# Projections out by one level of Strassen's algorithm, with their weight sums made by accumulating transfers

## The chip, the core and the metric

The kernel runs as one program on one core of a Trainium2 chip. The metric is the device time of one execution in microseconds. Five engines work side by side, each through its own list of instructions in order: TensorE (PE, with weight loads shown as PEld), VectorE (DVE), ScalarE (ACT), GpSimd (POOL) and SyncE (SP). They wait for each other by semaphores. In the kernel before, all transfers between HBM and the on-chip memory are issued by SP; a transfer that has to wait for a semaphore holds up all that SP issues behind it.

## The reference

Two layers over a sequence of 1024 tokens with 1024 features, all in float32:

```
layer 0 (mLSTM):      proj = x @ w_in  ->  xm, o_pre, z, gates        # inner width E = 2048, 4 heads
                      xc = silu(causal conv of xm); q, k from xc, v from xm; h = mLSTM cell
                      y = (sigmoid(o_pre) * norm(h) * gn_w + skip * xc) * silu(z)
                      branch = y @ w_out                               # 1024x2048 @ 2048x1024
layer 1 (short conv): bg, cg, hx, z = split(x @ w_in);  y = silu(z) * bg * conv(cg * hx)
                      branch = y @ w_out
both layers:          x = LayerNorm(ALPHA * x + branch) * g + b        # ALPHA = 4 ** 0.25
                      x = x + sigmoid(x @ W_g) * (p @ W_p)
```

The change is about the two products `y @ w_out`, one per layer, and about what stands on both sides of them.

## The kernel before

Features lie on the 128 partitions, tokens on the free axis in two halves of 512. A tile is 128x512 float32 (256 KB), and comes from one pool of slots whose names begin with the stage's name: `xm`, `oz` and `at` (layer 0: values and convolution, gates o and z, cell), `outa` (projection out), `ga` (embedding gate), then `b`, `outb`, `gb` for layer 1. A name with P in front is a bank of PSUM.

Every float32 operand is split into two fp32r parts: ACT rounds it (L67, "CAST"), DVE subtracts the rounded part (L70, "TENSOR_TENSOR"). A product is three matmuls (`three`, L80, L81, L82).

The order of the work is written out by hand, as one Python program over generators that are stepped at fixed places. Weights of all stages stand in one `stream`; `take` gives the next one and runs ahead with loads and splits by as many as `ahead` says. Heads 0 to 3 follow each other: value projection and convolution (L346, L365, L367), products O and Z of the gates (L549 to L553), the cell in chunks (L450 loads a row of maxima, L458 and L463 decays, L478 to L485), the norm of the cell. `apply_gates` (L560 to L565) loads `xc` back from HBM (`xcdram`), applies skip and gates, and stores `y` to `ydram`; it runs for `held` items when a head's norm has been drained.

`project` (outa, outb) takes a half of the tokens, then each column half: 16 k-tiles of y and of the weight, four banks, 4 x 16 x 3 matmuls, and adds ALPHA times the residual on eviction (L683). `layer_norm` sums over features by POOL additions (L659, L661) and by matmuls with a matrix of ones (L693); it is stepped inside the next half's projection. `gated` computes per tile of 128 features the gate (8 k-tiles), then the embedding product (2 k-tiles), then sigmoid (L784), product and sum (L785, L786). In `ga` each result goes to `keep`, which stores it and makes the operands of stage b.

Stage b, the input projection of layer 1, is already done by Strassen's algorithm in Winograd's form: seven products instead of eight for a 2x2 block product. Its 32 groups of weight rows each have seven products of 4 tiles x 3 matmuls; the weights' sums are made by DVE (L866), the moving operands' sums by `keep` (L819). Products are `a11`, `a12`, `s2`, `s1`, `s3`, `s4`, `a22`; their moving operands are called `n11`, `b21`, `t2`, `t1`, `n3`, `n22`, `n4`. `prepare_products` loads and splits three products ahead (`LEAD`), and starts when stage b starts. `outb` starts its loads when b is over (`fence`: they read what b stores).

Of the kernel before, what the change touches and what calls it, by code (L numbers as in the profile page):

```python
# [13 lines left out]
P = 128  # L14
# [16 lines left out]
AHEAD = {"load": 4, "split": 2}  # L31
LATE = {"load": 4, "split": 2}
# [4 lines left out]
def trunk(ctx: ExitStack, tc: tile.TileContext, I, out: bass.AP):  # L37
# [47 lines left out]
    ydram = dr.tile([16, 2, P, HALF], F32, name="ydram")  # L85
    ybdram = dr.tile([16, 2, P, HALF], F32, name="ybdram")
    mdram = dr.tile([32, P], F32, name="mdram")
    x2dram = dr.tile([8, 2, P, HALF], F32, name="x2dram")

# [13 lines left out]
    for h in range(2):  # L103
        for c in range(2):
            for k in range(16):
                if c == 0:
                    stream.append(("ya", ydram[k, h]))
                stream.append(("woa", I["woa"][cols(k), cols(c, HALF)]))
    for h in range(2):
        for c in (range(8) if h == 0 else ORDER):  # L110
            stream += [("wga", I["wga"][c, j]) for j in range(2)]
    for h in range(2):
        for c in range(2):
            for k in range(16):
                if c == 0:
                    stream.append(("yb", ybdram[k, h]))
                stream.append(("wob", I["wob"][cols(k), cols(c, HALF)]))
# [5 lines left out]
    fence = [[what for what, _ in stream].index("yb")]  # L123
# [228 lines left out]

    for hd in range(HEADS):
# [188 lines left out]
        def project_gates(c, mid):  # L542
# [3 lines left out]
            for h in range(2):  # L546
# [3 lines left out]
                mid()  # L550
                acc = in_group(wz, xsplit, h, mid)
# [3 lines left out]
                mid()  # L555

        def apply_gates(c, h, so, sz):
# [7 lines left out]
            nc.sync.dma_start(ydram[ct, h], sz)  # L565

        held = []

# [71 lines left out]
        if hd == HEADS - 1:  # L640
            ahead.update(load=16, split=3)

        def settle():
            if not step(side) and held:
                apply_gates(*held.pop(0))
# [4 lines left out]
        for item in held:  # L650
            apply_gates(*item)
# [11 lines left out]
    def project(h, ysp, wkind, residual, r, total):  # L663
        ysplit = [None] * 16
        for c in range(2):
            res = []
            acc = [bank() for _ in range(4)]
            for k in range(16):
                if c == 0:
                    ysplit[k] = ysp(k)  # L670
                wh, wl = take(wkind)
                if k == 8:
                    for t in range(4):
                        x = slot()
                        nc.sync.dma_start(x, residual(4 * c + t, h))
                        res.append(x)
                for t in range(4):
                    three(acc[t], (wh[:, cols(t)], wl[:, cols(t)]), ysplit[k], k == 0, k == 15)
                if c == 1:
                    ysplit[k] = None  # L680
                yield
            for t in range(4):
                nc.vector.scalar_tensor_tensor(out=res[t], in0=res[t], scalar=ALPHA, in1=acc[t],  # L683
                                               op0=ALU.mult, op1=ALU.add)
                r.append(res[t])
                summed(total, res[t])

    def summed_rows(stationary, x):
        parts = split(x, "act", "dve")
        yield  # L690
        acc = bank()
        for n in range(2):
            mm(acc, stationary, parts[n], start=(n == 0), stop=(n == 1))  # L693
        return acc

    def layer_norm(layer, h, r, total, x, xs):
        mu = yield from summed_rows(mean, total[1])
# [8 lines left out]
        for _ in range(3):  # L706
            yield
        var = bank()
        for j in range(4):
            mm(var[:, cols(j, 4)], squares[1][:, cols(j)], ones[:, :4], start=True, stop=True)  # L710
        rt = small([P, 4], "rt")
        nc.vector.tensor_scalar(out=rt, in0=var[:, :16].rearrange("p (j c) -> p j c", c=4)[:, :, 0],
                                scalar1=1.0 / DM, scalar2=LN_EPS, op0=ALU.mult, op1=ALU.add)
        nc.gpsimd.tensor_tensor(out=rt, in0=rt, in1=mhalf, op=ALU.pow)
        diag = slot()
# [3 lines left out]
        for _ in range(2):  # L719
            yield  # L720
        rs = yield from summed_rows(onesr, diag)
        yield
# [30 lines left out]
    def both_halves(layer, ysp, wkind, residual, late, early):  # L753
        x, xs = grid(8, 2), grid(8, 2)
        rs, totals = [[], []], [[], []]
        for n, _ in enumerate(project(0, ysp(0), wkind, residual, rs[0], totals[0])):
            if n == 29:
                early()
        side = layer_norm(layer, 0, rs[0], totals[0], x, xs)
        for n, _ in enumerate(project(1, ysp(1), wkind, residual, rs[1], totals[1])):  # L760
            if n % 2:
                step(side)
            if n >= 20:
                step(late)
        drain(side)
        drain(late)
        return x, xs, layer_norm(layer, 1, rs[1], totals[1], x, xs)

    def gated(layer, wkind, x, xs, pw, pt, side, emit):

        more = second_pt(layer, pt)
        for h in range(2):
            for c in (range(8) if h == 0 else ORDER):
                w = take2(wkind)
                acc = in_group(w, xs, h, lambda: step(side))
                step(side)
# [21 lines left out]
    part[0] = "ga"  # L798

# [284 lines left out]
```

## Time and profile before

| what | value |
|---|---|
| median of 3 runs | 2012.98 us (2012.39 to 2015.74) |
| the profiled execution | 2014.51 us, span 2012.7 us, mean granted clock 0.992 |
| PE busy | 1979.2 us, 98%, 8924 matmuls |
| DVE, ACT, POOL busy | 68%, 39%, 10% |
| layer 0 up to its projection out | 0 to 801.5 us |
| outa | 801.5 to 979.8 us |
| ga | 979.8 to 1099.8 us |
| b | 1099.8 to 1717.1 us |
| outb | 1717.1 to 1896.5 us |
| gb | 1896.5 to 2012.7 us |

The stages overlap on the other engines; the borders are those of PE's first matmul of each. A row of a group gives busy time and mean duration of one instruction, then the idle time before it and what ended it. A row of waits reads "engine, line, what it waited for: us in total, times, longest". A row of a window reads "from:to, length, then busy time and count of PE, PEld, DVE, ACT and POOL, PE's granted clock, busy share of the DMA engines, GB/s". A row of the timeline reads "start, duration, engine, line, operation, output<-input, shapes, count [idle before, and what ended it]". A row of DMA issues gives the median time from issue to landing.

### The profile page before, as it was taken

Reading aid. Unit: us, or ns where it says so; the run is one execution under the profiler, and the core shown is the slowest. Engines: PE = TensorE matmul, PEld = TensorE weight load, DVE = VectorE, ACT = ScalarE, POOL = GpSimd, SP = SyncE. Lnnn points to the kernel's source line nnn. Section 1 sums busy time; section 2 is a strip of 40 time slices with the busy share of each in tenths; the row PEclk is TensorE's granted clock in tenths of the full one; section 3 lists DMA queues with packets and bytes.
Section 4 is the critical chain, followed back from the end, with each engine's and each line's share of the span. In section 5 each row is a group of like instructions: output and inputs, shape, how many; then the busy total and the mean of one; then the engine's idle time right before and its main releaser. Section 6 shows DMA issues by size and latency. Waiting matters only on the chain.

```text
span 2012.7 us, 24481 instructions
## 1 busy us (share of the span) xinstructions
PE 1979.2 (98%) x8924; PEld 1631.9 (81%) x8924; DVE 1376.3 (68%) x2310; ACT 778.5 (39%) x1433; POOL 194.8 (10%) x154
## 2 busy tenths in 40 slices
PE   9999999999999999999998999999999999899998
PEld 6788878878887888887886888888888888787887
DVE  7974897589659965636777676676676676537663
ACT  5453235333433443514454333333333323514451
POOL 0210012001201120012300000000000000013200
PEclk9999999999999999999999999999999999999999
DMA  4111311232122123845023212211221220944222
GB/s 155 59 32 64 115 53 32 81 101 64 30 93 101 42 69 133 306 144 165 32 94 126 71 55 66 87 58 58 85 67 53 89 69 16 355 152 143 69 82 84
DMA packets 106058, 188.70 MB, mean 94 GB/s; under 512 B 11441, under 2 KB 15697, under 8 KB 105937
## 3 DMA queue, kind: packets, MB, share of 16 engines
q1 hardware_dynamic: 105936, 187.14, 28.1%
q8 instruction: 70, 1.15, 0.2%
q14 instruction: 52, 0.42, 0.1%
HBM read 153.52 MB, written 33.57 MB: 93 GB/s over the span
## 4 chain that ended last, share of the span: by engine, by line
PE 94%; DVE 4%; DMA 1%; issue 1%; ACT 0%; SPq 0%; DVEq 0%; ACTq 0%
PE Pb L80 10%; PE Pb L81 10%; PE Pb L82 10%; PE Poz L82 5%; PE Poz L80 5%; PE Poz L81 5%; PE Pat L80 3%; PE Pat L82 3%; PE Pat L81 3%; PE Poutb L80 3%; PE Poutb L82 3%; PE Pouta L82 3%; PE Poutb L81 3%; PE Pouta L80 3%; PE Pouta L81 3%; PE Pxm L80 3%
## 5 line engine op out<-in xcount | busy, mean ns | idle before, releaser
L80 PE MATMUL Pb<-ga,b 128*128 128x512 f32 x896 | 349.8, 390 | 6.8 <-ACT b L67 6.8
L81 PE MATMUL Pb<-ga,b 128*128 128x512 f32 x896 | 349.6, 390 | 0.0
L82 PE MATMUL Pb<-ga,b 128*128 128x512 f32 x896 | 347.1, 390 | 0.0
L80 PEld LDWEIGHTS Pb<-ga,b 128*128 128x128 f32 x896 | 168.7, 188 | 41.9 <-ACT b L67 7.2
L82 PEld LDWEIGHTS Pb<-ga,b 128*128 128x128 f32 x896 | 168.6, 188 | 35.2 <-DVE b L70 0.4
L81 PEld LDWEIGHTS Pb<-ga,b 128*128 128x128 f32 x896 | 168.6, 188 | 34.9
L70 DVE TENSOR_TENSOR b<-b,b 128x512 fp32r<-128x512 f32 x224 | 148.6, 687 | 60.5 <-ACT b L67 59.3
L67 ACT CAST b<-b 128x512 fp32r<-128x512 f32 x224 | 130.3, 616 | 113.9 <-DVE b L866 112.7
L911 ACT ACTIVATE b<-Pb 128x512 f32<-128x512 f32 x96 | 57.4, 598 | 203.3 <-PE Pb L82 203.3
L82 PE MATMUL Poz<-start,oz 128*128 128x512 f32 x288 | 115.8, 402 | 6.1 <-DVE oz L70 6.0
L80 PE MATMUL Poz<-start,oz 128*128 128x512 f32 x288 | 116.5, 404 | 0.0
L81 PE MATMUL Poz<-start,oz 128*128 128x512 f32 x288 | 115.2, 400 | 0.0
L80 PE MATMUL Poutb<-outb,outb 128*128 128x512 f32 x256 | 100.8, 394 | 6.3 <-ACT outb L67 6.3
L67 ACT CAST outb<-outb 128x512 fp32r<-128x512 f32 x116 | 67.2, 618 | 88.0 <-POOL outb L661 38.7
L82 PE MATMUL Poutb<-outb,outb 128*128 128x512 f32 x256 | 100.5, 393 | 0.7 <-DVE outb L70 0.7
L81 PE MATMUL Poutb<-outb,outb 128*128 128x512 f32 x256 | 100.4, 392 | 0.0
L82 PE MATMUL Pouta<-outa,outa 128*128 128x512 f32 x240 | 93.9, 391 | 0.8 <-DVE outa L70 0.8
L80 PE MATMUL Pouta<-outa,outa 128*128 128x512 f32 x240 | 93.7, 390 | 0.0
L81 PE MATMUL Pouta<-outa,outa 128*128 128x512 f32 x240 | 93.5, 390 | 0.0
L70 DVE TENSOR_TENSOR outb<-outb,outb 128x512 fp32r<-128x512 f32 x116 | 83.0, 763 | 13.3 <-ACT outb L67 13.0
L964 DVE TENSOR_TENSOR b<-Pb,b 128x512 f32<-128x512 f32 x32 | 22.1, 691 | 101.3 <-PE Pb L82 101.3
L67 ACT CAST outa<-outa 128x512 fp32r<-128x512 f32 x100 | 57.0, 618 | 81.9 <-POOL outa L661 38.7
(356 smaller groups left out, 4462.2 us busy)
## 6 DMA issues: line engine op xcount, KB each, us to landing
b<-wb SPq DMA_DIRECT2D x128, 256.0 KB, 2.9
outb<-wob SPq DMA_DIRECT2D x64, 256.0 KB, 5.3
outa<-woa SPq DMA_DIRECT2D x56, 256.0 KB, 3.8
oz<-wa SPq DMA_DIRECT2D x48, 256.0 KB, 3.6
xm<-wa SPq DMA_DIRECT2D x32, 256.0 KB, 3.0
oz<-xcdram SPq DMA_DIRECT2D x32, 256.0 KB, 3.0
ydram<-oz SPq DMA_DIRECT2D x32, 256.0 KB, 2.0
ybdram<-b SPq DMA_DIRECT2D x32, 256.0 KB, 2.1
```

The lines of the kernel that those rows point to most:

```text
L67: nc.scalar.copy(hi, src)
L70: (nc.vector if lo_on == "dve" else nc.gpsimd).tensor_tensor(out=lo, in0=src, in1=hi.bitcast(F32), op=ALU.subtract)
L80: mm(acc, lh, rh, start=first, stop=False, skip_group_check=onto)
L81: mm(acc, lh, rl, start=False, stop=False, skip_group_check=onto)
L82: mm(acc, ll, rh, start=False, stop=last, skip_group_check=onto)
L911: nc.scalar.activation(t, src, AF.Copy, scale=scale)
L964: nc.vector.tensor_tensor(out=s.c22, in0=acc, in1=s.m5, op=ALU.add)
```

## The change

It does eight things.

1. Both projections out become one Strassen step over 2x2 blocks: token halves, column halves of the weight, and even and odd k-tiles. Class `Out` runs 7 x 8 units of 4 tiles x 3 matmuls (56 units instead of 64), loading four units ahead and splitting two ahead.
2. Their weight sums s1 to s4 are made ahead by `weight_sums`: SP loads one term into a slot, GpSimd adds the other by an accumulating transfer (`add_on`), SP stores the sum to `wsdram`, and `Out` loads it from there. For layer 0 this runs during the O and Z products of heads 1 and 2 (two steps after each half), for layer 1 one step per group of stage b.
3. The moving operands' sums are made by DVE where y is made (`store_moving`), and all seven are stored.
4. The products are added up partly by DVE from PSUM into the residual (`onto`), partly by accumulating transfers between slots. The factor ALPHA moves into 1/ALPHA on the product and into the norm's epsilon.
5. `keep` makes t1 and n4 by accumulating transfers. In all 96 transfers accumulate (two times 32 for weight sums, two times 12 in the projections, 8 in `keep`).
6. The norm's waits are set by a table (`NORM_WAITS`); the embedding products of a half are computed in one block ahead of its gates and evicted by ACT, instead of after each gate.
7. Stage b begins with the first two products of four groups instead of two; its first products, and the first units of both projections, are loaded and split during the stage before.
8. A head's held gates are applied as soon as their part of the norm is there (`apply_ready`).

With it PE's list has 8650 rows instead of 8842, DVE's 2392 instead of 2304, ACT's 1477 instead of 1379, POOL's 255 instead of 159, SP's 925 instead of 717.

The first place is SP's list in head 1, between the last products O and Z before the cell and the cell itself. Before:

```order
L388 DMA xcdram<-xm_2582 128x512
L388 DMA xcdram<-oz_2656 128x512
L450 DMA oz_2814<-mdram 128x4x128
L450 DMA oz_2825<-mdram 128x4x128
L130 DMA at_3258<-wa 128x512
```

And now (L147 loads a term of a sum, L139 stores a sum, L516 is the store to `xcdram`, L578 the load of the maxima):

```order
L516 DMA xcdram<-oz_2693 128x512
L147 DMA oz_2748<-woa 128x512
L147 DMA oz_2749<-woa 128x512
L147 DMA oz_2750<-woa 128x512
L139 DMA wsdram<-oz_2747 128x512
L139 DMA wsdram<-oz_2749 128x512
L139 DMA wsdram<-oz_2748 128x512
L578 DMA oz_2862<-mdram 128x4x128
L578 DMA oz_2873<-mdram 128x4x128
L139 DMA wsdram<-oz_2750 128x512
L256 DMA at_3311<-wa 128x512
```

Three loads and three stores of the sums stand ahead of the cell's first load; the third store is that of s2, which has s1 added to it.

The second place is DVE's list at the boundary of heads 1 and 2. Before (L562 and L564 apply skip and gate, L346 is the next head's convolution):

```order
L553 TENSOR_TENSOR oz_3664<-Poz_3703,oz_3664 128x512
L70 TENSOR_TENSOR xm_3743<-oz_3576,xm_3742 128x512
L70 TENSOR_TENSOR xm_3749<-oz_3582,xm_3748 128x512
L562 SCALAR_TENSOR_TENSOR oz_3663<-oz_3736,cpack,oz_3663 128x512
L564 TENSOR_TENSOR oz_3664<-oz_3664,oz_3663 128x512
L346 SCALAR_TENSOR_TENSOR xm_3781<-xm_3779,cpack,xm_3781 128x511
```

And now (L696 and L698 are the skip and the gate, L94 the sums of `store_moving`, L72 splits, L472 the convolution):

```order
L696 SCALAR_TENSOR_TENSOR oz_3769<-oz_3824,cpack,oz_3769 128x512
L698 TENSOR_TENSOR oz_3770<-oz_3770,oz_3769 128x512
L94 TENSOR_TENSOR oz_3829<-oz_3557,oz_3770 128x512
L94 TENSOR_TENSOR oz_3831<-oz_3557,oz_3452 128x512
L94 TENSOR_TENSOR oz_3833<-oz_3452,oz_3829 128x512
L94 TENSOR_TENSOR oz_3835<-oz_3699,oz_3833 128x512
L72 TENSOR_TENSOR xm_3850<-oz_3690,xm_3849 128x512
L72 TENSOR_TENSOR xm_3856<-oz_3696,xm_3855 128x512
L472 SCALAR_TENSOR_TENSOR xm_3888<-xm_3886,cpack,xm_3888 128x511
```

The four sums now stand between the last gate of a head and the splits and convolution of the next. What L696 reads (`oz_3824`) is a load from `xcdram` that stands in SP's list behind the stores of s1, s3 and s2 of the fourth set.

The third place is ACT's list at the entry into stage b. Before, the first weights' casts (`b_`) stand behind the last gate's work (L784 the sigmoid, L812 a negated operand):

```order
L784 ACTIVATE ga_9707<-Pga_9675 128x512
L67 CAST ga_9716<-ga_9714 128x512
L67 CAST ga_9722<-ga_9712 128x512
L67 CAST ga_9726<-ga_9720 128x512
L812 ACTIVATE ga_9730<-ga_9707 128x512
L67 CAST b_9750<-b_9734 128x512
L67 CAST b_9754<-b_9736 128x512
```

And now (L977 the sigmoid; the first row is the cast of the first weight of stage b, among the last three gates):

```order
L69 CAST ga_9883<-ga_9867 128x512
L69 CAST ga_9887<-ga_9824 128x512
L69 CAST ga_9893<-ga_9830 128x512
L977 ACTIVATE ga_9922<-Pga_9897 128x512
L69 CAST ga_9932<-ga_9929 128x512
```

The cast of the first weight now stands ahead of the sigmoid of the third gate from the end, not behind the last gate's work. The diff, cut to what it is about:

```diff
+INV = 1.0 / ALPHA
+EARLY_GROUPS = 4
...
-    ydram = dr.tile([16, 2, P, HALF], F32, name="ydram")
-    ybdram = dr.tile([16, 2, P, HALF], F32, name="ybdram")
+    ydram = dr.tile([2, 7, 8, P, HALF], F32, name="ydram")
+    wsdram = dr.tile([2, 4, 8, P, HALF], F32, name="wsdram")
...
+    def add_on(dst, src):
+        nc.gpsimd.dma_start(dst, src, accum_op=ALU.add)
...
+    FRESH = ("a11", "a12", "s1")
+    def store_moving(layer, kk, y11, y12, y21, y22):
+        n3 = combined(y12, y22, ALU.subtract)
+        t1 = combined(y12, y11, ALU.subtract)
+        t2 = combined(y11, n3, ALU.subtract)
+        n4 = combined(y21, t2, ALU.subtract)
+        for n, y in enumerate((y11, y21, t2, t1, n3, y22, n4)):
+            nc.sync.dma_start(ydram[layer, n, kk], y)
...
+    def weight_sums(layer, weights):
+        rows = lambda k, i: weights[cols(k), cols(i, HALF)]
+        store = lambda n, kk, t: nc.sync.dma_start(wsdram[layer, n, kk], t)
+        s4 = None
+        for kk in range(8):
+            if s4 is not None:
+                store(3, kk - 1, s4)
+            s1, s2, s3, s4 = (slot() for _ in range(4))
+            for t, src in ((s1, rows(2 * kk, 1)), (s2, rows(2 * kk, 0)), (s3, rows(2 * kk, 0)),
+                           (s4, rows(2 * kk + 1, 0))):
+                nc.sync.dma_start(t, src)
+            yield
+            add_on(s1, rows(2 * kk + 1, 1))
+            add_on(s3, rows(2 * kk, 1))
+            yield
+            add_on(s2, s1)
+            store(0, kk, s1)
+            store(2, kk, s3)
+            s1 = s3 = None
+            yield
+            add_on(s4, s2)
+            store(1, kk, s2)
+            s2 = None
+            yield
+        store(3, 7, s4)
...
+        UNITS = ([("a11", kk) for kk in range(6)] + [("a12", kk) for kk in range(6)]
+                 + [("a11", 6), ("a11", 7), ("a12", 6), ("a12", 7)]
+                 + [(what, kk) for what in ("s2", "s3", "a22", "s1", "s4") for kk in range(8)])
+        LOADS, LEAD = 4, 2
...
+        def load(self, n):
+            while self.loaded < min(n, len(self.UNITS)):
+                for dst, key, src in self.loads[self.loaded]:
+                    dst[key] = slot()
+                    nc.sync.dma_start(dst[key], src)
+                self.loaded += 1
...
+                what, kk = self.UNITS[self.prepared]
+                left = split(self.w.pop((what, kk)), "act", "dve")
+                m = MOVING[what]
+                y = self.y.pop((m, kk))
+                self.ready[what, kk] = left, split_negative(y) if m in NEGATIVE else split(y, "act", "dve")
...
+            for u, (what, kk) in enumerate(self.UNITS):
+                if kk == 7:
+                    continue
+                before(u)
+                self.load(u + 1 + (kk == 6) + self.LOADS)
+                self.prepare(u + 1 + (kk == 6) + self.LEAD)
+                acc = banks(what, kk == 0)
+                for t in range(4):
+                    one(what, kk, t)
+                    if kk == 6:
+                        one(what, 7, t)
+                        after(what, t)
+                        tick()
+                    elif t % 2:
+                        tick()
+                for n in (6, 7) if kk == 6 else (kk,):
+                    del self.ready[what, n]
...
+                if (hd, c, h) == (HEADS - 1, CTH - 1, 1):
+                    outa.prepare(3)
...
+                if hd in (1, 2):
+                    step(sums, 2)
+                if hd == HEADS - 1 and c >= CTH - 2:
+                    outa.load((2, 3, 5, 5)[2 * (c - CTH + 2) + h])
...
-            nc.sync.dma_start(ydram[ct, h], sz)
+            paired[c, h] = sz
+            pair = [(k, l) for k in (c - c % 2, c - c % 2 + 1) for l in range(2)]
+            if all(key in paired for key in pair):
+                store_moving(0, ct // 2, *(paired.pop(key) for key in pair))
...
+        def apply_ready():
+            for n, (c, h, _, _) in enumerate(held):
+                if hnt[h][c] is not None:
+                    apply_gates(*held.pop(n))
+                    return
...
-            if not step(side) and held:
-                apply_gates(*held.pop(0))
+            step(side)
+            apply_ready()
...
+    NORM_WAITS = ((1, 3, 8, 2, 3), (1, 2, 2, 1, 1))
...
+        def onto(r, acc, scale):
+            nc.vector.scalar_tensor_tensor(out=r, in0=acc, scalar=scale, in1=r, op0=ALU.mult, op1=ALU.add)
...
+        def after(what, t):
+            if what == "a11":
+                kept[t] = evacuated(b["b1"][t], -INV)
+            elif what == "a12":
+                r = out_.x[t, 0]
+                onto(r, b["b3"][t], INV)
+                add_on(r, kept.pop(t))
+                b["b3"][t] = None
+            elif what == "s2":
+                result(t, 0)
+                add_on(out_.x[t, 1], evacuated(b["b1"][t], -INV))
+            elif what == "s3":
+                add_on(out_.x[t + 4, 1], evacuated(b["b1"][t], INV))
+            elif what == "a22":
+                add_bank(t + 4, 0, b["b1"][t], INV)
+                b["b1"][t] = None
+            elif what == "s1":
+                add_bank(t + 4, 1, b["b2"][t], INV)
+            else:
+                add_bank(t, 1, b["b2"][t], -INV)
+                b["b2"][t] = None
+        def tick():
+            place[0] += 1
+            if side:
+                step(side[0])
+            elif place[0] >= 2 * 24 and place[0] % 2:
                 step(late)
-        drain(side)
+        out_.run(banks, before, tick, after)
         drain(late)
-        return x, xs, layer_norm(layer, 1, rs[1], totals[1], x, xs)
-
-    def gated(layer, wkind, x, xs, pw, pt, side, emit):
+        return x, xs, side
...
+            embedding = []
+            for c in range(8):
                 pp = bank()
                 for k in range(2):
                     wh, wl = pw[2 * k + c // 4]
                     three(pp, (wh[:, cols(c % 4)], wl[:, cols(c % 4)]), pt[h][k], k == 0, k == 1)
-                step(side)
+                embedding.append(evacuated(pp))
+                del pp
+                if h == 0 and c % 2 == 0:
+                    (fetch if c == 0 else prepare)((4, 2, 3, 4)[c // 2])
+                step(norms[h])
+                if h == 0 and c % 2:
+                    step(norms[1])
+            pt[h].clear()
+            drain(norms[h])
+            if h:
+                pw.clear()
+            for n, c in enumerate(range(8) if h == 0 else ORDER):
...
+            negative[c] = slot()
+            nc.scalar.activation(negative[c], x2, AF.Copy, scale=-1.0)
         elif c < 4:
-            t1 = difference(x2, raw2[k][0])
-            ops["t1"][k] = split(t1, "act", "dve")
+            add_on(negative[k], x2)
+            finish_operands()
...
+            add_on(negative[k + 4], t2)
             ops["t2"][k] = split(t2, "act", "dve")
-            n4 = difference(raw2[k + 4][0], t2)
+            ops["t1"][k] = split(negative.pop(k), "act", "dve")
...
+            def last():
+                ops["n4"][k] = split_negative(negative.pop(k + 4))
+            late.append(last)
...
+        made[c, h] = y
+        if c % 2 and h == 0:
+            store_moving(1, c // 2, *(made.pop((k, h)) for k in (c - 1, c) for h in range(2)))
...
+    def hook(n):
+        if n >= 5:
+            prepare_products(n - 4)
+    gated(0, "wga", x1, x1s, pw, pt, side, keep, hook)
+    part[0] = "b"
+    outb = Out(1, I["wob"], lambda k, h: x2dram[k, h])
+    sums = weight_sums(1, I["wob"])
...
+        if g == len(groups) - 1:
+            outb.load(1 + n)
+            outb.prepare(max(0, n - 3))
         product(g, n)
+        if n == 3 and 0 < g:
+            step(sums)
+    drain(sums)
```

More of the change, by code (lines that the diff above doesn't have):

```diff
@@ L661, in summed, with over_rows @@
             nc.gpsimd.tensor_tensor(out=total[1], in0=total[1], in1=x, op=ALU.add)
[L663 to L690, printed above, removed]
+    def over_rows(stationary, parts):
         acc = bank()
@@ L694, in summed_rows, with waits @@
         return acc
+    NORM_WAITS = ((1, 3, 8, 2, 3), (1, 2, 2, 1, 1))
     def layer_norm(layer, h, r, total, x, xs):
-        mu = yield from summed_rows(mean, total[1])
+        def waits(n):
+            return range(NORM_WAITS[h][n])
+        for _ in waits(0):
+            yield
+        parts = split(total[1], "act", "dve")
+        total.clear()
+        for _ in waits(1):
+            yield
+        mu = over_rows(mean, parts)
+        del parts
         squares = []
@@ L705, in layer_norm @@
                 yield
-        for _ in range(3):
+        del mu
+        for _ in waits(2):
             yield
@@ L718, in layer_norm @@
                                 in1=rt.unsqueeze(2).to_broadcast([P, 4, P]), op=ALU.mult)
[L719 removed]
+        parts = split(diag, "act", "dve")
+        del diag
+        for _ in waits(4):
             yield
[L721 to L722 removed]
+        rs = over_rows(onesr, parts)
+        del parts
         for k in range(8):
@@ L751, in grid, with back, banks, result @@
         return [[None] * m for _ in range(n)]
-    def both_halves(layer, ysp, wkind, residual, late, early):
+    def back(layer, out_, before, late):
         x, xs = grid(8, 2), grid(8, 2)
[L755 to L761, printed above, removed]
-                step(side)
-            if n >= 20:
+        rs, totals, side = [{}, {}], [[], []], []
+        b, kept, place = {}, {}, [0]
+        BANK = {"a12": "b3", "s1": "b2", "s4": "b2"}
+        def banks(what, first):
+            name = BANK.get(what, "b1")
+            if first and what in FRESH:
+                b[name] = [bank() for _ in range(4)]
+            return b[name]
+        def onto(r, acc, scale):
+            nc.vector.scalar_tensor_tensor(out=r, in0=acc, scalar=scale, in1=r, op0=ALU.mult, op1=ALU.add)
+        def result(c, h):
+            r = rs[h][c] = out_.x.pop((c, h))
+            summed(totals[h], r)
+            if len(rs[h]) == 8:
+                side.append(layer_norm(layer, h, rs[h], totals[h], x, xs))
+        def add_bank(c, h, acc, scale):
+            onto(out_.x[c, h], acc, scale)
+            result(c, h)
+        def after(what, t):
[16 more added lines that the diff above has]
+                add_bank(t + 4, 1, b["b2"][t], INV)
+            else:
+                add_bank(t, 1, b["b2"][t], -INV)
[5 more added lines that the diff above has]
+            elif place[0] >= 2 * 24 and place[0] % 2:
@@ L994, in trunk @@
     fence[0] = len(stream)
-    ahead.update(load=16, split=4)
     pw, pt = [], ([], [])
-    x3, x3s, side = both_halves(1, lambda h: lambda k: take("yb"), "wob", lambda k, h: x2dram[k, h],
-                                ple_operands(1, pw, pt, 0), lambda: None)
+    x3, x3s, side = back(1, outb, lambda u: None, ple_operands(1, pw, pt, 0))
     ahead.update(load=4, split=2)
```

141 lines of the change are left out of this document (84 added, 57 removed).

## The prediction

> **What bounds the kernel now.** I read the page first, then the rows of each stretch, the list of PE's waits, the chain around the longest of them, and the DMA issues.
>
> ```profile
> PE 1979.2 (98%) x8924; PEld 1631.9 (81%) x8924; DVE 1376.3 (68%) x2310; ACT 778.5 (39%) x1433; POOL 194.8 (10%) x154
> PE 94%; DVE 4%; DMA 1%; issue 1%; ACT 0%; SPq 0%; DVEq 0%; ACTq 0%
> 1138.90:1700.10 561.20, 561.20 (x2477) 465.05 (x2477) 390.74 (x653) 182.59 (x324) 0.00 (x0) 1.00 0.21 68
> ```
>
> PE is busy 98% of the span and holds 94% of the chain that ended last. The third row is the undisturbed part of stage b: 561.20 us for 2477 matmuls, so a 128x512 matmul advances the end by 561.20/2477 = 0.2266 us. The 390 ns that the groups give as a mean overlap, and are no cost. The kernel therefore takes its matmuls times 0.2266 us plus the places where PE stands still. Those are few:
>
> ```profile
> PE Pb L80 <- ACT b L67: 6.8, 1, 6.8
> PE Poutb L80 <- ACT outb L67: 6.3, 1, 6.3
> PE Poz L82 <- DVE oz L70: 6.0, 3, 2.0
> PE Pouta L82 <- DVE outa L70: 1.0, 3, 0.4
> PE Poutb L82 <- DVE outb L70: 0.7, 2, 0.4
> ```
>
> The columns are total us, times, longest. The first two are the entries into b and outb, the third the three boundaries between heads. All other stages, both projections out included, run at PE's pace.
>
> **Fewer matmuls.** A projection out is now 2 halves x 2 column halves x 16 k x 4 tiles x 3 = 768 matmuls of 128x512. With seven products it is 7 x 8 x 4 x 3 = 672. Two layers: 192 fewer, 192 x 0.2266 = **-43.5 us**. The gates keep their 192 matmuls per half and the embedding its 48; those only stand in another order. Nothing hides this term as long as PE stays the bound there.
>
> **The two entries.** The chain of waits there:
>
> ```profile
> 1092.86 0.24 PE Pga L82
> ...
> 1099.28 0.52 ACT b L67
> ...
> 1099.84 0.80 PE Pb L80
> 1100.63 0.43 PE Pb L81
> ...
> 1712.53 3.86 DMA outb<-wob
> ...
> 1717.09 0.80 PE Poutb L80
> 1717.88 0.43 PE Poutb L81
> ```
>
> Into b, the last gate's result goes through DVE and ACT, and only behind that does ACT cast the first weights. PE stands 6.8 us, and its next five matmuls take 0.43 instead of 0.23 us, 1.6 us with the first one's 0.80. Into outb a weight load is issued only when everything before it is over; 6.3 us, and 1.9 us behind it in the same way. After the change three units of weights are loaded and split ahead at both places, 3 x 12 x 0.2266 = 8.2 us of matmuls that wait for nothing new, and b's first eight products (four groups, a11 and a12: 8 x 12 x 0.2266 = 21.8 us) need only n11 and b21, which the gates of the first half make. I take both as gone: 6.8 + 1.6 + 6.3 + 1.9 = **-16.6 us**. If the cover were short, at most these 16.6 come back.
>
> **The norm.** The mean's sums wait twice in each layer (last two rows, 0.4 at the longest). Placed later by the new pacing they go: 1.0 + 0.7 and their slower restart, **-2 us**. Norm 0 now lies inside the 16 units of s1 and s4, 43.5 us. Per 96 matmuls (21.8 us) the densest part of the new order gives DVE 29 operations of 128x512.
>
> ```profile
> 801.54:979.81 178.27, 177.27 (x781) 145.64 (x780) 101.60 (x152) 73.40 (x130) 27.31 (x19) 1.00 0.55 182
> L70 DVE TENSOR_TENSOR outa<-outa,outa 128x512 fp32r<-128x512 f32 x100 | 70.8, 777 | 7.4 <-ACT outa L67 7.4
> ```
>
> The first row is outa (DVE 101.6 of 178.3 us), the second its splits, 777 ns each. 29 x 0.777 = 22.5 us against 21.8: 0.7 us too much, with a lead of two units (5.4 us) that absorbs it once but not where waits for POOL's sums fall into it. Bounds: 0 with all absorbed, 4 us a layer if the windows beside it (26 operations, 20.2 us) lose two waits of 0.7 each as well. I take 1.5 a layer, **+3 us**.
>
> **The tail.** The embedding's six matmuls (1.4 us) stood behind the last gate and covered its sigmoid. Now the sigmoid stands bare ahead of
>
> ```profile
> 2007.80 0.70 DVE gb L785
> 2008.52 0.69 DVE gb L786
> ```
>
> ACT's 0.6 us and the hand-overs: **+0.8 us**.
>
> **The weight sums.** This is the part whose price the trace does not have. No row of the kernel before is an accumulating transfer, and no transfer starts on GpSimd. Let A be the time from the start of one such 256 KB transfer to its landing. The nearest rows:
>
> ```profile
> b<-wb SPq DMA_DIRECT2D x128, 256.0 KB, 2.9
> outb<-wob SPq DMA_DIRECT2D x64, 256.0 KB, 5.3
> oz<-xcdram SPq DMA_DIRECT2D x32, 256.0 KB, 3.0
> ydram<-oz SPq DMA_DIRECT2D x32, 256.0 KB, 2.0
> outa<-woa SPq DMA_DIRECT2D x56, 256.0 KB, 3.8
> oz<-mdram SPq DMA_DIRECT2D x8, 256.0 KB, 4.2
> ```
>
> From below 2.9, a load in a quiet stage. From above 5.3 + 2.0 = 7.3, a load in the busiest stage and then a store, since what is added to is read and written again. I take the 5.3 between.
>
> The Trainium skill ("DMA: Bandwidth & Descriptors", section "Anatomy of one DMA — SWDGE (gpsimd) path") gives 2.0 us plus bytes over 436 GB/s for a transfer that GpSimd issues, so an estimate of 2.6 us for this size. No run here shows it; with it the two terms below would be zero.
>
> In b a step of the sums comes once in a group (38 us), and a store never waits for an add of its own step: no cost. In heads 1 and 2 two steps come together, so SP issues a store that waits for an add just begun, and everything behind it in SP's order waits too.
>
> Place one is the entry into the cells of heads 1 and 2:
>
> ```profile
> 301.13 0.33 SPq L388 DMA_DIRECT2D xcdram<-oz  x1
> 304.28 1.24 SPq L450 DMA_DIRECT2D oz<-mdram  x2
> ...
> 315.50 0.62 ACT L480 CAST at<-at 128x512 fp32r<-128x512 f32 x1 [0.76 <-DVE at L478]
> ...
> 317.96 0.44 PE L80 MATMUL Pat<-oz,at 128*128 128x512 f32 x1
> ```
>
> Behind the xcdram store at 301.13 SP now issues the loads of s2, s3, s4 (0.4 each), which land 3.8 later, 305.7; GpSimd then adds s1 onto s2, and its store (306 + A) stands before the mdram loads, which land 4.2 and some issue later, 311 + A. ACT began on them at 313.55, and its product has 317.96 - 316.12 = 1.8 us to spare. Stall: 311 + A - 313.5 - 1.8, about A - 4; 1.3 us a head at 5.3.
>
> Place two is the boundary behind heads 1 and 2:
>
> ```profile
> 419.18 2.32 DVE L346 SCALAR_TENSOR_TENSOR xm<-xm,cpack,xm 128x511 f32<-128x511 f32 x3 [2.83 <-ACT xm L376]
> ...
> 440.42 0.69 DVE L387 TENSOR_TENSOR xm<-xm,xm 128x512 f32<-128x512 f32 x1 [0.76 <-ACT xm L381]
> ...
> 452.94 0.50 PE L82 MATMUL Poz<-start,oz 128*128 128x512 f32 x1 [2.01 <-DVE oz L70]
> ```
>
> From the next head's first convolution (419.18) DVE runs with 0.76 us idle until a split for which PE already waits 2.01 us (452.94). So whatever delays that convolution by more than 0.76 goes into the span. In the new order the third set's loads are issued 186 matmuls ahead of that point, at 419.18 - 42.2 = 377.0, and land at 380.8; three adds, each waiting for the one before (380.8 + 3A); the fourth set's first load (1.7 for issue, 3.8 to land), two more adds (386.3 + 5A); two issues and the xcdram load behind them (0.8 + 3.0), then on DVE two operations of the gate, four of store_moving and two splits (5.5) before the convolution: 395.6 + 5A against 419.94. At 5.3: 2.2 us a head; nothing below 4.9. Together 2 x (1.3 + 2.2) = 7 us, and the matmuls behind a stop of 2 us cost another 1.4 each time as at the entries: **+10 us**.
>
> The other side of the two bounds is 0 at A = 2.9 and 2 x (3.3 + 12.1) + 3 = 34 us at 7.3.
>
> Another rule of the Trainium skill speaks against this change ("SBUF — State Buffer", section "Who interferes with whom"): operations of DVE in a two-port mode, tensor_scalar among them, lock GpSimd out while it writes its descriptors. The page reports a transfer of 620 ns that took 3100. No run here shows it; by it A would be longest exactly at place two, where such operations stand in rows.
>
> **The sum.** The profiled execution has a span of 2012.7 us (2014.51 around it; the median of the runs is 2012.98). 2012.7 - 43.5 - 16.6 - 2 + 3 + 0.8 + 10 = 1964.4, so a median of about **1965 us**.
>
> **Rivals.** (1) *The sums are hidden.* A below 4.9 and DVE never late: 1964.4 - 10 - 3 = **1951**. For it speak the 2.9 and 3.0 of the loads in quiet stages; against it, that the sums read two sources and that DVE's part of place two (5.5 us) is longer than the 2.83 idle there. (2) *Slow sums.* A from 6.5 to 9: each further us costs 2 x (5 + 1) = 12, so from 1954.4 + 12A - 56.6 + 3 **1979 to 2008**. (3) *Sums so slow that the change loses.* One mechanism: SP stands in order behind stores that wait for adds, at the two places. What the change gains without it is 2012.7 - 1954 = 58 us; 2 x (A - 4 + 5A - 24.3) = 58 at A = 9.6. Beyond that it is slower, at 10.5 **2024**. Each add would have to take a third longer than the 7.3 of the upper bound. (4) *DVE becomes the bound of the projections.* The products need two splits per unit of 2.7 us, four sums per pair and the norm. If DVE is late through all of s1, s4 and the embedding, two layers lose about 10 us each: **1980**. Against it: 101.6 of 178.3 us busy now, and only one window of 21.8 us is over full. (5) *The entries stay.* Splits stand ahead, but ACT or DVE still works off the last gate first: up to 16.6 back, **1981**.
>
> **Chances.** Forecast (1956 to 1976) 0.47; rival 1 0.25; rival 2 0.10; rival 3 0.05; rival 4 0.07; rival 5 0.06. The likeliest gives 1965. Range: rival 1 less the 4 us that its terms may be off, 1947, up to 1990, which leaves out rival 3 and the upper half of rival 2. Faster or slower means by more than 0.2% (4 us), about what a measurement of this kernel can tell from no change. Faster 0.92, same 0.02, slower 0.06.
>
> **What would show it.** Right: the projections out take about 153 us each at 0.2266 per matmul; no wait of PE at the entries into b and outb; DMA issues of the sums with a median A between 4 and 6.5; waits of PE on ACT or DVE at the entries into the cells and after the boundaries of heads 1 and 2 that grew by 1 to 4 us, with none at head 3. Wrong: a wait of PE on a load inside the projections, DVE busy over 95% of a slice there, A under 4 (then 1951) or over 7, or a stall in b next to a store of sums.

## The result, and the profile after

The changed kernel takes 1981.2 us (median of 4 runs, 1977.3 to 1983.5), beside 2012.9 for the kernel before: a ratio of 0.984, 95% interval 0.982 to 0.986. The forecast was faster, 1965, with a range of 1947 to 1990. So the direction and the range held, but of the 48 us forecast 32 came. The profiled execution of the changed kernel has a span of 1977.7 us (1979.65 around it). The kernel before, run beside each experiment, had medians from 2012.9 to 2015.0; each ratio is to the one beside it, and a difference of 2 us between the medians of two experiments says nothing by itself.

The page of the changed kernel, its engines and the shares of the chain of waits:

```profile
PE 1940.3 (98%) x8732; PEld 1597.1 (81%) x8732; DVE 1439.1 (73%) x2398; ACT 826.4 (42%) x1529; POOL 292.6 (15%) x250
PE 76%; DVE 14%; DMA 3%; issue 3%; ACT 2%; SPq 1%; POOL 0%; DVEq 0%; POOLq 0%; ACTq 0%
```

PE has 192 matmuls fewer and is still busy 98%, but holds only 76% of the chain that ended last (94% before); DVE has 14%, DMA 3%. The waits of PE in the same execution:

```profile
PE Poz L82 <- ACT oz L69: 8.2, 3, 3.3
PE Pat L82 <- ACT at L608: 6.1, 2, 3.1
...
PE Pb L82 <- ACT b L69: 3.3, 1, 3.3
PE Pga L809 <- ACT ga L69: 2.1, 1, 2.1
PE Pouta L83 <- DVE outa L72: 1.2, 3, 0.6
...
PE Poutb L83 <- DVE outb L72: 1.0, 2, 0.6
PE Poutb L809 <- DVE outb L72: 0.7, 2, 0.5
PE Pouta L809 <- DVE outa L72: 0.7, 2, 0.5
```

The wait at the entry into outb (6.3) is gone. The one into b has halved, from 6.8 to 3.3. The three waits at the boundaries between heads have grown from 6.0 to 8.2. Two waits in the cells of heads 1 and 2 are new (6.1), and so is one for the second norm's result (2.1).

To see where the time is, I take the time between the first matmuls of two stretches and subtract the stretch's own matmuls at 0.22656 us per 512 columns. What is left is lost there, idle or at half pace. "Start" goes from PE's first matmul to the first cell, "heads" from there to outa; the 1.2 us before the first matmul are in no row. For the profiled executions, in us:

| stretch | before | changed | t1, n4 by DVE | late casts | lead 6 and 4 | stores by GpSimd | late casts, lead, stores |
|---|---|---|---|---|---|---|---|
| matmuls | 1920.1 | 1876.6 | 1876.6 | 1876.6 | 1876.6 | 1876.6 | 1876.6 |
| start | 17.0 | 17.1 | 15.5 | 17.8 | 17.3 | 17.1 | 15.9 |
| heads, all | 41.4 | 51.7 | 51.0 | 52.3 | 50.4 | 41.4 | 40.8 |
| of it the cells of heads 1 and 2 | 9.1 | 18.9 | 14.4 | 18.5 | 14.0 | 9.0 | 9.1 |
| outa | 3.4 | 5.0 | 5.0 | 5.0 | 2.8 | 5.0 | 2.9 |
| ga | 10.4 | 5.8 | 5.3 | 5.5 | 5.8 | 6.0 | 5.7 |
| b | 8.3 | 8.2 | 2.6 | 1.5 | 8.6 | 8.6 | 1.4 |
| outb | 4.5 | 5.0 | 5.0 | 5.0 | 2.8 | 5.0 | 2.8 |
| gb | 6.5 | 7.1 | 7.1 | 7.2 | 7.1 | 7.1 | 7.1 |
| span | 2012.7 | 1977.7 | 1969.2 | 1972.0 | 1972.7 | 1968.0 | 1954.4 |

In the kernel before, the idle time at the entry into b (6.9) stands at the end of ga and the half-pace matmuls behind it (1.5) in b; that at the entry into outb (6.5) at the end of b and in outb (1.8). The change takes away 43.5 of matmuls and 8.6 at the two entries (7.5 at outb, 1.1 at b), and adds 10.3 in the heads, 6.1 around the norms and 0.7 at the two ends.

What an accumulating transfer takes, from issue to landing, the row of DMA issues of the changed kernel:

```profile
oz<-woa POOLq DMA_DIRECT2D x16, 256.0 KB, 4.6
oz<-oz POOLq DMA_DIRECT2D x16, 256.0 KB, 4.4
...
b<-wob POOLq DMA_DIRECT2D x16, 256.0 KB, 5.5
b<-b POOLq DMA_DIRECT2D x16, 256.0 KB, 3.8
...
outa<-outa POOLq DMA_DIRECT2D x12, 256.0 KB, 7.8
...
outb<-outb POOLq DMA_DIRECT2D x12, 256.0 KB, 7.7
...
ga<-ga POOLq DMA_DIRECT2D x8, 256.0 KB, 5.1
```

These are medians, of 3.8 to 7.8 us; in the heads, where the prediction's A counted, 4.4 and 4.6, with single transfers from 3.3 to 6.4.

### The profile page after: what moved, and what is told of

The parts are those of the page before. It is cut to its first block, busy times and chain, and to the rows that moved or that the text cites. A ratio compares the mean times of both kernels' runs of the same rounds, so it can differ in the third digit from the quotient of the medians.

```text
span 1977.7 us, 24966 instructions
## 1 busy us (share of the span) xinstructions
PE 1940.3 (98%) x8732; PEld 1597.1 (81%) x8732; DVE 1439.1 (73%) x2398; ACT 826.4 (42%) x1529; POOL 292.6 (15%) x250
## 4 chain that ended last, share of the span: by engine, by line
PE 76%; DVE 14%; DMA 3%; issue 3%; ACT 2%; SPq 1%; POOL 0%; DVEq 0%; POOLq 0%; ACTq 0%
PE Pb L84 10%; PE Pb L82 10%; PE Pb L83 10%; DVE xm L495 4%; PE Poz L82 4%; PE Poz L84 4%; PE Poz L83 3%; PE Pat L82 3%; PE Pat L84 3%; PE Pat L83 3%; DVE xm L472 2%; PE Poutb L83 2%; PE Pouta L83 2%; PE Poutb L84 2%; PE Pouta L84 2%
## 5 line engine op out<-in xcount | busy, mean ns | idle before, releaser
L82 PE MATMUL Pb<-ga,b 128*128 128x512 f32 x852 | 332.8, 391 | 3.3 <-ACT b L69 3.3
L83 PE MATMUL Pb<-ga,b 128*128 128x512 f32 x852 | 332.4, 390 | 0.0
L84 PE MATMUL Pb<-ga,b 128*128 128x512 f32 x852 | 329.2, 390 | 0.5 <-DVE b L72 0.5
L82 PEld LDWEIGHTS Pb<-ga,b 128*128 128x128 f32 x852 | 160.7, 189 | 37.0 <-ACT b L69 3.8
L84 PEld LDWEIGHTS Pb<-ga,b 128*128 128x128 f32 x852 | 160.5, 188 | 34.8 <-DVE b L72 1.4
L83 PEld LDWEIGHTS Pb<-ga,b 128*128 128x128 f32 x852 | 160.7, 189 | 33.3
L72 DVE TENSOR_TENSOR b<-b,b 128x512 fp32r<-128x512 f32 x218 | 145.6, 684 | 34.0 <-ACT b L69 32.9
L72 DVE TENSOR_TENSOR outa<-outa,outa 128x512 fp32r<-128x512 f32 x107 | 76.9, 771 | 27.4 <-ACT outa L69 27.1
L72 DVE TENSOR_TENSOR outb<-outb,outb 128x512 fp32r<-128x512 f32 x104 | 75.1, 772 | 26.8 <-ACT outb L69 25.4
L83 PE MATMUL Pouta<-outa,outa 128*128 128x512 f32 x212 | 83.0, 392 | 1.2 <-DVE outa L72 1.2
L83 PE MATMUL Poutb<-outb,outb 128*128 128x512 f32 x212 | 83.0, 392 | 1.2 <-DVE outb L72 1.0
L111 POOL DMA_DIRECT2D b<-wob x16 | 13.9, 870 | 468.6 <-PE Pb L84 352.9
L84 PE MATMUL Poutb<-outb,outb 128*128 128x512 f32 x212 | 82.4, 390 | 0.0
L84 PE MATMUL Pouta<-outa,outa 128*128 128x512 f32 x212 | 82.4, 389 | 0.0
L1053 DVE TENSOR_TENSOR b<-b,b 128x512 f32<-128x512 f32 x116 | 77.1, 684 | 0.5
L472 DVE SCALAR_TENSOR_TENSOR xm<-xm,cpack,xm 128x511 f32<-128x511 f32 (+2 forms) x96 | 75.0, 783 | 0.9 <-ACT xm L504 0.6
```

The source lines that it names most:

```text
L72: (nc.vector if lo_on == "dve" else nc.gpsimd).tensor_tensor(out=lo, in0=src, in1=hi.bitcast(F32), op=ALU.subtract)
L82: mm(acc, lh, rh, start=first, stop=False, skip_group_check=onto)
L83: mm(acc, lh, rl, start=False, stop=False, skip_group_check=onto)
L84: mm(acc, ll, rh, start=False, stop=last, skip_group_check=onto)
L111: nc.gpsimd.dma_start(dst, src, accum_op=ALU.add)
L472: nc.vector.scalar_tensor_tensor(out=dst[:, d:], in0=src[:, :HALF - d], scalar=tap, in1=dst[:, d:], op0=ALU.mult, op1=ALU.add)
```

## The experiments

### The entry into b

In the changed kernel the chain into the stall, and ACT's timeline beside it:

```profile
1090.49 5.18 DMA ga<-ga
...
1097.36 0.52 ACT b L69
1097.88 0.04 issue
1097.92 0.79 PE Pb L82
1098.72 0.43 PE Pb L83
```

```profile
1088.24 0.63 ACT L104 ACTIVATE ga<-ga 128x512 fp32r<-128x512 f32 x1 [2.17 <-DMA ga<-ga]
...
1093.68 0.62 ACT L69 CAST ga<-ga 128x512 fp32r<-128x512 f32 x1 [3.81 <-DVE ga L94]
1095.69 1.14 ACT L69 CAST ga<-ga 128x512 fp32r<-128x512 f32 x2 [1.39 <-DMA ga<-ga]
...
1097.27 0.60 ACT L69 CAST b<-ga 128x512 fp32r<-128x512 f32 x1
```

`DMA ga<-ga` is an accumulating transfer of `keep`, which makes t1 or n4. ACT stands 2.17 and 1.39 us at casts of what such transfers make, and 3.81 us between them for DVE's sums of the last gate (L94). The cast of b's next weight (`b<-ga`) stands behind all of these in its list. PE runs out of prepared weights and waits; its next 13 matmuls, most of them at 0.43, take 6.0 us in place of 2.9.

The first experiment makes t1 and n4 on DVE:

```diff
-            negative[c] = slot()
-            nc.scalar.activation(negative[c], x2, AF.Copy, scale=-1.0)
...
-            add_on(negative[k], x2)
+            negative[k] = combined(x2, raw2[k][0], ALU.subtract)
...
-            add_on(negative[k + 4], t2)
+            negative[k + 4] = combined(raw2[k + 4][0], t2, ALU.subtract)
...
-                ops["n4"][k] = split_negative(negative.pop(k + 4))
+                ops["n4"][k] = split(negative.pop(k + 4), "act", "dve")
```

> The changed kernel with t1 and n4 of stage b's operands made by two subtractions on DVE instead of a negated copy on ACT and an accumulating transfer; 88 accumulating transfers are left. Theory: PE's wait at the entry into b (3.3 us and 13 matmuls at half pace, 7.2 us in all) comes from ACT, whose list stands behind casts that wait for those transfers, so the weights' casts behind them are late. Then that wait falls under 1 us, the entry costs under 3 us, and the time falls by 4 to 6 us to about 1976. Rival: the last gate's own work on DVE and ACT sets the entry, with or without transfers; then the wait stays within 1 us of 3.3, or grows with the eight more subtractions, and the time stays at 1981.

Measured: 1973.7 us, 0.980 of the kernel before (0.979 to 0.982). No wait of PE on ACT for b is left in the profile, and b loses 2.6 us instead of 8.2. It takes away two things at once, though: the transfers, and eight negated copies on ACT. So a second one keeps both, and only puts the eight splits of t1 and n4 off into the first products of b:

```diff
-            finish_operands()
...
-            ops["t1"][k] = split(negative.pop(k), "act", "dve")
+            def first():
+                ops["t1"][k] = split(negative.pop(k), "act", "dve")
+            late.insert(k, first)
...
-        if i in (2, 4):
+        if 2 <= i < 10:
             finish_operands()
```

> The changed kernel with the accumulating transfers and the negated copies of stage b's operands kept, and only the eight splits of what they make (t1 and n4) put off into the first products of stage b. It tells apart what the run with DVE's subtractions changed together. Theory: ACT standing at casts that wait for transfers is the whole entry; then PE's wait of 3.3 us at the entry goes here too and the time falls by 4 to 6 us to 1976. Rival: the eight negated copies on ACT or the transfers' traffic made the weights late; then the wait stays above 2 us and the time stays at 1981.

Measured: 1973.4 us, ratio 0.980 (0.979 to 0.982), b loses 1.5 us. PE has no wait at the entry, although ACT still stands there for DVE's sums of the last gate:

```profile
1092.22 1.14 ACT L69 CAST ga<-ga 128x512 fp32r<-128x512 f32 x2 [2.94 <-DVE ga L94]
```

So the last gate's own work is covered by the prepared products; what was not covered was the place of the casts of t1 and n4 in ACT's list, and it is neither the copies nor the transfers as such. How much of it was ACT's standing and how much the casts' own time ahead of the weights, no run separates.

The entry alone, put into the kernel before:

```diff
-    for g in range(0, 2):
+    for g in range(4):
         order += [(g, 0), (g, 1)]
...
+    def hook(n):
+        if n >= 5:
+            prepare_products(n - 4)
+
+    gated(0, "wga", x1, x1s, pw, pt, side, keep, hook)
```

> The kernel before with one part of the change alone: stage b begins with two products of four groups, and its first three weights are loaded and split during the last three gates of the stage before; no accumulating transfer, no Strassen step in the projections out. If loading and splitting ahead is enough, as the prediction had it, the wait of 6.8 us on ACT goes and 8 us with it: 2004.5. If the last gate's work on ACT and DVE stands in the way by itself, a wait of 3 us or more stays and the time is above 2009.

Measured: 2006.6 us beside 2015.0 for the kernel before, ratio 0.996 (0.995 to 0.998), 8.4 us less (5 to 11 by the interval). Of the two entries, the list of waits has only the untouched one:

```profile
PE Poutb L80 <- ACT outb L67: 6.6, 1, 6.6
```

So loading and splitting ahead is worth about what the prediction said, 8 us; in the changed kernel the splits of t1 and n4 took most of it back.

### The sums in heads 1 and 2

The changed kernel at the cell of head 1. SP's timeline (start in us, length, instruction):

```profile
303.00 1.39 SPq L147 DMA_DIRECT2D oz<-woa  x3
304.48 9.66 SPq L139 DMA_DIRECT2D wsdram<-oz  x3
314.24 1.00 SPq L578 DMA_DIRECT2D oz<-mdram  x2
```

GpSimd's at the same time, and the chain behind it:

```profile
308.50 0.89 POOL L111 DMA_DIRECT2D oz<-woa  x1 [3.49 <-DMA oz<-woa]
309.09 1.21 POOL L111 DMA_DIRECT2D oz<-oz  x1
314.09 0.88 POOL L111 DMA_DIRECT2D oz<-oz  x1 [3.80 <-DMA oz<-oz]
```

```profile
314.24 4.15 DMA oz<-mdram
318.45 1.28 ACT L591
...
322.36 0.80 PE Pat L82
323.16 0.43 PE Pat L83
```

SP has issued three loads and then spends 9.66 us over three stores. Its waits between 304 and 315 us say at which of them:

```profile
SPq L139 <- DMA oz<-woa: 7.4, 1, 7.4
SPq L139 <- DMA oz<-oz: 1.0, 1, 1.0
```

`DMA oz<-woa` is the add that makes s3, `DMA oz<-oz` the one that makes s2. SP stands 7.4 us at the second store, that of s3: GpSimd first waits for the load of s3 and starts its add at 308.50, which lands at 312.4. Only 1.0 us more is for s2, whose add starts at 309.09 and lands at 313.8. Then the loads of the maxima are issued, at 314.24 instead of about 305. In head 2 the two waits are 7.7 and 0.9. PE waits 3.1 us, and loses another 1.7 in seven matmuls at half pace.

The first try was to move the store of s2 in the program:

```diff
+                store(1, kk - 1, s2)
                 store(3, kk - 1, s4)
...
-            store(1, kk, s2)
...
+        store(1, 7, s2)
```

> The changed kernel with one store of the weight sums moved: s2 is stored with s4 at the beginning of the next set, not right behind the add that makes it. Theory: the cells of heads 1 and 2 start late because SP stands at that store in front of the loads of the maxima; without it PE's two waits of 3.0 and 3.1 us in the cells go with the half-pace matmuls behind them, 9.9 us in all, to about 1971. Rival: the loads are late because of the transfers' traffic or GpSimd's order, not of SP's; then waits of more than 2 us stay there and the time stays above 1977.

Measured: 1982.3 us, as the changed kernel. It says nothing about the theory, because SP's list did not change. The order within a list is made by the framework, and the store still stands ahead of the maxima; SP's list of this experiment has

```
L139 DMA wsdram<-oz_2748 128x512
L578 DMA oz_2862<-mdram 128x4x128
L578 DMA oz_2873<-mdram 128x4x128
L139 DMA wsdram<-oz_2750 128x512
```

and its timeline the same standstill:

```profile
302.82 9.16 SPq L139 DMA_DIRECT2D wsdram<-oz  x3
```

The run is therefore a repetition of the changed kernel, and shows that the share of the loss between the cells and the boundaries differs from execution to execution (cells 15.7 here, 18.9 there), while the heads together lose 51.2 and 51.7. It was also aimed at the lesser of the two stores: with that of s3 left in place, SP would have stood 7.4 of the 8.4 us all the same.

The second try gives the stores to the engine that makes the sums:

```diff
-        store = lambda n, kk, t: nc.sync.dma_start(wsdram[layer, n, kk], t)
+        store = lambda n, kk, t: nc.gpsimd.dma_start(wsdram[layer, n, kk], t)
```

> The changed kernel with the 64 stores of weight sums issued by GpSimd, which makes the sums, instead of by SP; SP's list then has the loads of the maxima directly behind the loads of the sums' terms, and nothing of SP's waits for an accumulating transfer of the sums. Theory: the two cells' late start is SP standing at those stores; PE's waits on ACT in the cells (3.0 and 3.1 us) go with their half-pace matmuls, and the time falls by 7 to 10 us, to 1971 to 1974. Rival: traffic, or GpSimd's own order (its splits of head values now stand behind stores too), holds the heads back: the cells stay over 2 us late or the boundaries grow by as much, and the time is 1978 or more.

Measured: 1969.1 us, ratio 0.978 (0.977 to 0.979), 12 us less than the changed kernel. PE has no wait in the cells any more, and the heads lose 41.4 us, as much as before the change. The loads, the adds and the stores are all still there; only SP no longer stands behind them, and issues the first load of the maxima at 305.31.

And without the sums of layer 0 at all. The projection then loads plain weights in their place, so this kernel leaves out what the sums are for:

```diff
-    sums = weight_sums(0, I["woa"])
+    sums = iter(())
...
-                if what in SUMS:
+                if what in SUMS and layer:
```

> The changed kernel with the weight sums of layer 0 left out: no loads, adds or stores of them in heads 1 and 2, and the projection of layer 0 loads plain weights in their place, so its numbers are not the reference's. It prices the sums by themselves: the prediction's term was 10 us, the profile of the changed kernel shows 10.4 more lost in the heads than before. If the sums are the whole cause, the heads lose 30 us again as in the kernel before and the time falls by 10 to 1971. If the new order of DVE's work (the four sums of store_moving, the earlier gates) has a part, the heads keep 2 us or more of it and the time stays above 1973.

Measured: 1968.2 us, ratio 0.977 (0.976 to 0.979). The heads lose 39.6. Two of its boundaries differ by 1.6 us for another reason: behind a wait of the same length the granted clock falls in one place and not in the next. The stretches behind these waits, of 2.33 and 2.29 us (PE's clock is the number ahead of the last two):

```profile
482.70:486.10 3.40, 3.40 (x11) 2.82 (x12) 3.40 (x5) 1.32 (x3) 2.27 (x1) 0.50 0.12 45
677.70:681.10 3.40, 3.40 (x17) 2.85 (x18) 3.40 (x5) 1.47 (x3) 2.29 (x1) 1.00 0.16 61
```

The first boundary loses 5.4 us, the second 3.8. Within this spread, stores on GpSimd are as good as no sums, and no cost of the new order of DVE's work there (`store_moving`, gates applied earlier) is seen.

### The norms in the projections out

```diff
-        LOADS, LEAD = 4, 2
+        LOADS, LEAD = 6, 4
```

> The changed kernel with units of the projections out loaded six ahead instead of four and split four ahead instead of two. Theory: the small waits of PE on DVE in s1 and s4 (0.6, 0.6 and so on; 4.9 us lost in outa, 5.0 in outb against 3.4 and 2.7 before) come from bursts of the norm in DVE's list, which a longer lead absorbs: 2 to 4 us less, 1978. Rival: DVE is full over the whole of s1 and s4, or the waits are those of the norm's own matmuls; then no lead helps and the time stays within 1 us.

Measured: 1977.6 us, ratio 0.981 (0.980 to 0.983), 3.6 less. The rows show it more surely than the medians: outa and outb lose 2.8 each instead of 5.0, less than before the change. What is left of waits there is for the norm's own matmul:

```profile
PE Pouta L809 <- ACT outa L69: 1.4, 1, 1.4
PE Poutb L809 <- ACT outb L69: 1.4, 1, 1.4
```

So DVE was late in bursts, not full: in the changed kernel it is busy for all of the 7 us from 934 to 941, and PE's two waits for it there (0.5 and 0.6) end at 934.28 and 941.09. The wait for the second norm in ga (`PE Pga L809`, 2.1 us) is the same in this run and in the run with late casts. With t1 and n4 on DVE, which takes eight copies off ACT, it is 1.1, but then PE waits 2.4 us on ACT in the gates of ga (0.5 in the changed kernel). Nothing was tried that aims at it.

### The three together

> The changed kernel with three edits together: t1 and n4 by DVE, the lead of six and four units, and the sums' stores on GpSimd. If the three causes are separate, their gains add: about 7 + 4 + 8 us, so 1962. If the stores on GpSimd bring nothing, 1970.

Measured, with t1 and n4 on DVE: 1959.7 us, ratio 0.973 (0.971 to 0.975). The gains add: 7.5 + 3.6 + 12.1 = 23.2 by themselves, 21.5 together, within what the medians can tell.

> The version with all three edits, with the late splits in place of DVE's subtractions. If the two ways of mending the entry are worth the same it is within 2 us of 1960; if the subtractions on DVE had cost something that was hidden in the entry, it is 1956 or less.

Measured, with late casts in place of the subtractions: **1956.2 us**, ratio 0.972 (0.970 to 0.973), 25 us under the changed kernel and 57 under the one before. The intervals of the two versions overlap, so no difference between the two ways of mending the entry is shown. The longest waits of PE in the second:

```profile
PE Poz L82 <- ACT oz L69: 7.0, 3, 2.3
PE Poz L427 <- DVE bs L424: 4.2, 1, 4.2
PE Pga L809 <- ACT ga L69: 2.1, 1, 2.1
PE Pxm L82 <- ACT start L69: 1.6, 1, 1.6
PE Pouta L809 <- ACT outa L69: 1.4, 1, 1.4
PE Poutb L809 <- ACT outb L69: 1.4, 1, 1.4
```

The start and the boundaries between heads stood in the kernel before too.

## Why the prediction was right or wrong

**Fewer matmuls, -43.5.** Right: the matmuls of the trace come to 43.5 us less, and the projections take their matmuls plus 5.0 us each.

**The two entries, -16.6.** Half of it failed, and this is the step that cost most. outb came as predicted: 7.5 of 8.2. At b 1.1 of 8.4 came. The cover was counted in matmuls of prepared weights, but the prediction did not look at what else stood in ACT's list: the casts of t1 and n4, which wait for transfers of 5.1 us. It named ACT's work off the last gate as the rival (entries stay, 1981), gave it 0.06, and had the wrong piece in mind: that the time came out at 1981 is no sign for this rival. The run with late casts shows the place of the casts in the list to be the cause, and the run on the kernel before shows that about 8 us were there to be had.

**The norm, -2 + 3.** The sign was right and the size was off: +6.1 instead of +1. The sums' waits did not go away; they came back as waits of 0.5 to 0.6 us on DVE in s1, and of up to 0.5 for the norm's own matmuls in s4. A burst of 0.7 us too much per 21.8 us had been seen, and a lead of two units was trusted to absorb most of it. Four units do. The 2.1 us wait for the second norm in ga was not foreseen.

**The tail, +0.8.** gb lost 0.6 more: right.

**The sums, +10.** The total was right (10.3 in the heads) and its parts were not. A was 4.4 and 4.6 at the median and 4.7 for the add of s2 that counted, not far from the 5.3 taken. At place one, the cells, the loss was 4.8 and 5.1 each, not 1.3 (the sum's own terms give A - 4.3, so 1.0). The step that failed there is the wait: the prediction had SP stand for s2 alone. It stood for s3 first, since the store of s3 stands ahead of that of s2 and waits for an add that itself waits for its load. s2's add began at 309.1 rather than 306: the head ran 1.5 us later by then, the loads landed after 4.3 to 4.6 us rather than 3.8, and s3's add stands ahead in GpSimd's list. The half-pace matmuls of 1.7 us follow here too, while the sum had put them at the boundaries. At place two the next head's convolution is not delayed at all: it starts at 425.05, 5.87 us later than before, and the head's first product, at 418.11, is later by the same 5.87 (DVE's timeline of the changed kernel):

```profile
425.05 2.32 DVE L472 SCALAR_TENSOR_TENSOR xm<-xm,cpack,xm 128x511 f32<-128x511 f32 x3
```

The three boundaries lost 0.9 and 0.6 more and 1.1 less than before in this execution, not 2.2 and 1.4 each. The chain of five adds does not exist: the third set's adds were over before SP came to their stores, because SP was held by a store of y until 385.7 (SP's timeline of the changed kernel, in us of start and length),

```profile
385.67 2.25 SPq L134 DMA_DIRECT2D ydram<-oz  x2
...
411.10 5.60 SPq L139 DMA_DIRECT2D wsdram<-oz  x3
416.75 0.42 SPq L694 DMA_DIRECT2D oz<-xcdram  x1
```

and of the fourth set two adds in a row delay the load behind them, for which DVE then stands 0.17 us at 419.80. That two errors of about the same size and opposite sign made the term come out is luck. In the five profiled executions with SP's stores the heads lost 9.0 to 10.9 us more than before, of it the cells 4.9 to 9.8.

**The price of a transfer.** The medians here are 3.8 us at the least, the shortest single transfer 3.3. The fit of the Trainium skill ("DMA: Bandwidth & Descriptors", section "Anatomy of one DMA — SWDGE (gpsimd) path") gives 2.6 for this size and does not hold for these transfers. The lock-out of GpSimd by DVE's tensor_scalar rows, as the Trainium skill has it ("SBUF — State Buffer", section "Who interferes with whom"), was hardly put to the test: of the 32 adds in the heads four start beside such a row (377.83, 378.47, 578.19 and 578.83). GpSimd was busy with starting them for 1.1 to 1.5 us instead of 0.9 (1.2 for one behind another without such rows), and they landed after 4.3 to 5.7 us, where the other adds from HBM (`oz<-woa`) took 3.9 to 4.9. If that is the lock-out, it cost by these numbers about 1 us at most; no run shows whether it is. The add that held the cells had no such row beside it.

**The rivals.** All hidden (1951) put its condition on A below 4.9, and the medians in the heads met it (4.4 and 4.6), yet 10.3 us were lost there, where the sum's terms give about 1 at such an A: it had the order of SP's waits wrong, not the price of a transfer. With the three lists mended the kernel is at 1956, so about this time was there to be had. Slow sums were not the case, since they begin at 6.5. DVE as the bound of the projections was not the case either, since a longer lead mends it.

## What to carry to other kernels

Before work is called hidden, read the whole list of the engine that must deliver it: one instruction that waits for a transfer holds up all that stands behind it, however idle the engine is. Where one engine starts a transfer and another must wait for it in the middle of its own list, give the dependent transfer to the engine that already waits; here that was worth 12 us. Where the framework orders the lists, look at the list again after an edit before the run is read as a test of it.

## What the runs showed of the hardware

In the changed kernel an accumulating transfer of 256 KB that GpSimd starts took 3.8 us (median of `b<-b`) to 7.8 (`outa<-outa`), single ones 3.3 to 9.5; plain loads by SP in the same two stages took 3.7 (`b<-wob`) and 5.3 (`outa<-ydram`). GpSimd is busy for 0.9 us with starting one. Plain stores of the sums that GpSimd starts took 3.7 us in the heads and 3.6 in b, where SP's of the same sums took 2.6 and 3.2 in the changed kernel. After a wait of PE of 2.3 us the granted clock was 0.5 for the next 3.4 us in one place and 1.0 in two others of the run without sums; after the three waits of 2.0 us in the kernel before it was 0.5 each time.
